# A residual that takes its natural row order by a trip through HBM, in a one-layer encoder kernel

## The chip, the cores and the metric

The kernel runs on one core of a Trainium2 chip. A core has TensorE (PE, matrix products; its weight loads are listed as PEld), VectorE (DVE), ScalarE (ACT), GpSimd (POOL) and SyncE (SP), which run at once, each through its own instructions in order, and tie to each other by semaphores. SBUF is the memory on the chip with 128 partitions, PSUM takes the products of TensorE, and DMA queues move data between SBUF and HBM. The metric is the time of one execution in microseconds on the device; less is better.

## The reference, cut to what matters

One layer: a mixing sub-layer (recurrent branch and attention, merged by gates), then a feed-forward sub-layer. What touches the change is the last part:

```python
mix_out = jnp.einsum("bsd,de->bse", merged, w_out[layer])
x = x + rms_norm(mix_out, mix_norm_post[layer])
h = rms_norm(x, ffn_norm_pre[layer])
up = jnp.einsum("bsd,df->bsf", h, w_up[layer])          # 1024 -> 2 x 3072
up = causal_dwconv(up, conv_f_w[layer], conv_f_b[layer])
gate, val = jnp.split(up, 2, axis=-1)
ffn_out = jnp.einsum("bsf,fd->bsd", jax.nn.gelu(gate) * val, w_down[layer])
x = x + rms_norm(ffn_out, ffn_norm_post[layer])
```

There are 512 tokens of width 1024, all in float32. Every norm is taken per token, so the order in which tokens lie in the partitions does not matter to it; the convolution runs along tokens and needs their order.

## The kernel before, in words

**Precision.** Every operand of a product is split into a rounded high half (written by ScalarE as a cast) and a low half (operand minus high half, mostly by VectorE). Three matmuls stand for one: high x high, high x low, low x high.

**Row order.** The host gives the tokens of each block of 128 in a turned order: partition a*64+i holds token 2i+a. All token-major tiles have that order, the residual `x2t` among them (four blocks of 128 tokens x 1024). Channel-major tiles come out of transposes; there the matmul reads its moving operand through `turns`, which restores the order of tokens. At the end the host puts the rows of the output back into natural order.

**Mixing, end.** `mix_norm` (L1232) takes one block of 128 tokens through the post-norm, adds the residual into `x2t` (L1247, VectorE) and goes on to the pre-norm of the feed-forward part. The blocks run at about 512 to 547 us.

**Up-projection** (about 566 to 757 us of the span). 24 pairs of weight tiles (one of the gate half, one of the value half). The first three are done plainly, the others with seven products in place of eight (a Strassen scheme), one pair per call of `period` (L480), some 9.4 us each. A pair's `raw_up` weights (2 x 512 KB) are loaded by SyncE's queue, L374, three pairs ahead (`load`, L1504). The low halves `ml` of its plain weights are made by a DMA: ScalarE writes the negated rounding (L390), and POOL's queue adds the weight to it (L391, an accumulating DMA, 512 KB for the first tile, 256 KB for half of the second). A load takes over the SBUF of the pair two before, so it waits until that pair's `ml` DMAs have landed. The product gate x value, `yf`, is made on POOL (L1378) and written to HBM as `yd` by SyncE's queue (L1379). The order within a period is written out by hand.

**Down-projection** (about 760 to 872 us). Again seven products in place of eight, of six steps each: 42 steps, each with two blocks of 128 tokens by two weight tiles, twelve matmuls of 512 columns. `prep(i)` (L1469) makes the four halves of step i: the weight's high half `wh_dn` on ScalarE (L198) and low half `wl_dn` on VectorE (L201), the gated product's high half `ah` on ScalarE (`y_hi`, L1464) and low half `al` on VectorE (`y_lo`, which goes through the helper `sub`, L351). It runs two steps ahead of `down_step` (L1478). From step 6 on the gated product's quarters `q` are combined by VectorE (L1574) first. In `y_hi` and `y_lo` the source is read through `parted`, which takes every second element, so that the product's columns, which are tokens, come into the turned order; then the output rows fit the order of `x2t`. The last product's second token block is done in halves of 256 columns.

**End.** Blocks of the result are folded together (L1605, L1688), squared and scaled, and `x2t` is added: for the blocks 2 and 3 by an accumulating DMA on POOL's queue (L1632), for the blocks 0 and 1 by VectorE (L1626). Then they go out.

Tile names end in running numbers, which the profile leaves out. A listing of instructions shows `ml_11` for the first low tile or the second of pair 11, by its size 128x1024 or 128x512.

Of the kernel before, what the change touches and what calls it, by code (L numbers as in the profile page):

```python
# [8 lines left out]
F32 = mybir.dt.float32  # L9
# [78 lines left out]
def kernel(  # L88
# [1111 lines left out]
    xpool = fstk.enter_context(tc.tile_pool(name="x2", bufs=1, reuse_waits="tile"))  # L1200
    x2t = xpool.tile([P, NT, D], F32, name="x2t")
    nc.sync.dma_start(x2t, xv)
    def out_matmuls(acc, toks, k, ah, al, wh, wl, nk, halves=(0, 1)):
        for t in toks:
            tok = slice(t * P, (t + 1) * P)
            for hf in halves:
                c = slice(512 * hf, 512 * hf + 512)
                dst = acc[t][hf]
                pe.matmul(dst, ah[:, tok], turns(wh[:, c], SH), start=k == 0, stop=False)
                pe.matmul(dst, ah[:, tok], turns(wl[:, c], SH), start=False, stop=False)  # L1210
                pe.matmul(dst, al[:, tok], turns(wh[:, c], SH), start=False, stop=k == nk - 1)
# [7 lines left out]
    with ExitStack() as mix:  # L1219
# [12 lines left out]
        def mix_norm(t, acc):  # L1232
            u = n2pool.tile([P, D], F32, tag="u", name=f"u{t}")
            xn = n2pool.tile([P, D], F32, tag="xn", name=f"xn2_{t}")
            s2 = small.tile([P, 2], F32, tag="s2", name=f"s2_mix{t}")
            for i, c in enumerate(HALVES):
                act.activation(out=xn[:, c], in_=acc[t][i], func=AF.Square, accum_out=s2[:, i : i + 1])
                dve.tensor_tensor(out=u[:, c], in0=acc[t][i], in1=gb[0][:, c], op=ALU.mult)
            yield
            ss = small.tile([P, 1], F32, tag="ss", name=f"ss_mix{t}")  # L1240
            dve.tensor_tensor(out=ss, in0=s2[:, 0:1], in1=s2[:, 1:2], op=ALU.add)
            rs = rstd_of(ss, f"mix{t}", eps4)
            if t > 1:
                yield
            s3 = small.tile([P, 2], F32, tag="s2", name=f"s2_f{t}")
            for i, c in enumerate(HALVES):
                dve.scalar_tensor_tensor(out=x2t[:, t, c], in0=u[:, c], scalar=rs, in1=x2t[:, t, c],  # L1247
                                         op0=ALU.mult, op1=ALU.add)
                act.activation(out=xn[:, c], in_=x2t[:, t, c], func=AF.Square, accum_out=s3[:, i : i + 1])
            yield  # L1250
            ss = small.tile([P, 1], F32, tag="ss", name=f"ss_f{t}")
            dve.tensor_tensor(out=ss, in0=s3[:, 0:1], in1=s3[:, 1:2], op=ALU.add)
            rs = rstd_of(ss, f"f{t}")
            for c in HALVES:
                scaled2[t] = dve.scalar_tensor_tensor(out=xn[:, c], in0=x2t[:, t, c], scalar=rs, in1=gb[1][:, c],
                                                      op0=ALU.mult, op1=ALU.mult)
            yield
            turned[t] = to_channels(xn, t, h2h, h2l, hf, "f")
# [195 lines left out]
        yraw[1, m] = ypool.tile([P, 2, SH], F32, tag="yr", name=f"yr{m}")  # L1454
        nc.sync.dma_start(yraw[1, m], yd[m][:, :, X])

    def tokens(y, order):
        return order(y.rearrange("p k c -> p (k c)"))

    def y_hi(i):  # L1460
        pl, b = (ypool, 3) if i < NS else (dpools[0], LATE)
        yhl[i] = [pl.tile([P, 2, SH], F32R, tag=f"a{x}", name=f"a{x}{i}", bufs=b) for x in "hl"]
        yhl[i].append(yraw[STEPS[i]])
        act.copy(tokens(yhl[i][0], placed), tokens(yhl[i][2], parted))  # L1464

    def y_lo(i):
        sub(tokens(yhl[i][1], placed), tokens(yhl[i][2], parted), tokens(yhl[i][0].bitcast(F32), placed))

    def prep(i):  # L1469
        if i < len(STEPS):  # L1470
# [31 lines left out]
    pairs.update({j: none for j in (JF, JF + 1, JF + 2)})  # L1502

    def load(j):  # L1504
        if NU < j < JF - 3:
            pairs[j + 3] = up_pair(j + 3)
        elif j == JF - 2:
            for i in range(2):
                load_w(i)
                load_first(i)  # L1510
# [286 lines left out]
```

## Time and profile before

| What | Value |
|---|---|
| median of three runs | 887.05 us (886.27 to 887.78) |
| the profiled execution | 886.33 us |
| its span | 884.6 us, 15833 instructions |
| PE, DVE, ACT, POOL busy | 98%, 84%, 69%, 24% of the span |
| DMA | 185.24 MB, 209 GB/s in the mean |

The span runs from the first to the last instruction; the execution's time has 1.7 us more. A group row ends in busy time, mean ns of one, idle time before and what ended it. A row of the timeline gives start, duration, engine, line, operation and tiles, and in brackets the engine's idle time ahead of it with what ended that. A DMA's time to landing runs from its issue to its semaphore. Ends of matmuls are modelled, so starts are compared here.

### The profile page before, as it was taken

Reading aid. Unit: us, or ns where it says so; the run is one execution under the profiler, and the core shown is the slowest. Engines: PE = TensorE matmul, PEld = TensorE weight load, DVE = VectorE, ACT = ScalarE, POOL = GpSimd, SP = SyncE. Lnnn points to the kernel's source line nnn. Section 1 sums busy time; section 2 is a strip of 40 time slices with the busy share of each in tenths; the row PEclk is TensorE's granted clock in tenths of the full one; section 3 lists DMA queues with packets and bytes.
Section 4 is the critical chain, followed back from the end, with each engine's and each line's share of the span. In section 5 each row is a group of like instructions: output and inputs, shape, how many; then the busy total and the mean of one; then the engine's idle time right before and its main releaser. Section 6 shows DMA issues by size and latency. Waiting matters only on the chain.

```text
span 884.6 us, 15833 instructions
## 1 busy us (share of the span) xinstructions
PE 871.0 (98%) x5856; PEld 794.5 (90%) x5856; DVE 744.6 (84%) x1209; ACT 611.1 (69%) x1031; POOL 215.4 (24%) x278
## 2 busy tenths in 40 slices
PE   9999999999999999999999999999999999999996
PEld 7888888888899988888888889999999999988885
DVE  7986469738978849998868699999999999889997
ACT  6575595533466648776755497888888888688774
POOL 3344334536011013121104100233332332100000
PEclk9999999999999999999999999999999999999999
DMA  7787689999874377353506663778898898699864
GB/s 268 231 273 220 172 228 258 238 277 197 192 182 135 116 261 274 132 171 129 202 26 202 218 200 107 175 183 236 217 222 244 211 226 208 223 399 307 276 192 149
DMA packets 71040, 185.24 MB, mean 209 GB/s; under 512 B 7153, under 2 KB 27681, under 8 KB 70578
## 3 DMA queue, kind: packets, MB, share of 16 engines
q1 hardware_dynamic: 47360, 127.72, 43.2%
q0 software_dynamic: 23456, 56.37, 29.3%
q8 instruction: 46, 0.75, 0.3%
q14 instruction: 32, 0.26, 0.1%
q10 hardware_dynamic: 146, 0.14, 0.0%
HBM read 150.69 MB, written 35.73 MB: 211 GB/s over the span
## 4 chain that ended last, share of the span: by engine, by line
PE 85%; DVE 9%; ACT 2%; issue 2%; DMA 1%; DVEq 0%; SPq 0%; ACTq 0%
PE up L458 7%; PE up L456 7%; PE up L455 7%; PE dn L1500 2%; PE dn L1499 2%; PE dn L1498 2%; PE ga L245 2%; PE ga L244 2%; PE ga L246 2%; DVE al L351 2%; PE pa L245 2%; PE pa L244 2%; PE v L335 2%; PE v L336 2%; PE xa L244 2%
## 5 line engine op out<-in xcount | busy, mean ns | idle before, releaser
L1370 DVE SCALAR_TENSOR_TENSOR u<-up,cpt,u 128x511 f32<-128x511 f32 x96 | 71.3, 745 | 3.5 <-ACT u L1364 1.8
L391 POOL DMA_DIRECT2D ml<-raw_up x42 | 36.2, 861 | 148.1 <-ACT ml L390 88.8
L1500 PE MATMUL dn<-wh_dn,al 128*128 128x512 f32 (+1 forms) x180 | 66.5, 369 | 1.2 <-DVE al L351 1.2
L1499 PE MATMUL dn<-wl_dn,ah 128*128 128x512 f32 (+1 forms) x180 | 66.2, 368 | 0.5 <-DVE wl_dn L201 0.4
L1498 PE MATMUL dn<-wh_dn,ah 128*128 128x512 f32 (+1 forms) x180 | 65.7, 365 | 0.0
L455 PE MATMUL up<-sh,th 128*128 128x256 f32 x252 | 59.5, 275 | 0.0
L456 PE MATMUL up<-sl,th 128*128 128x256 f32 x252 | 59.5, 275 | 0.0
L201 DVE TENSOR_TENSOR wl_dn<-raw_dn,wh_dn 128x1024 fp32r<-128x1024 f32 x42 | 51.1, 1217 | 5.0 <-ACT wh_dn L198 5.0
L351 DVE TENSOR_TENSOR tl<-t,th 128x1024 fp32r<-128x1024 f32 x42 | 51.1, 1218 | 0.0
L1364 ACT ACTIVATE u<-up,cpt 128x512 f32<-128x512 f32 x48 | 36.9, 778 | 19.9 <-PE up L458 10.0
L455 PEld LDWEIGHTS up<-sh,th 128*128 128x128 f32 x252 | 48.4, 192 | 0.0
L456 PEld LDWEIGHTS up<-sl,th 128*128 128x128 f32 x252 | 48.4, 192 | 0.0
L198 ACT CAST wh_dn<-raw_dn 128x1024 fp32r<-128x1024 f32 x42 | 44.3, 1054 | 4.7 <-DMA raw_dn<-td 2.8
L437 ACT CAST th<-t 128x1024 fp32r<-128x1024 f32 x42 | 43.8, 1045 | 2.6 <-DVE t L351 0.6
L1378 POOL TENSOR_TENSOR yf<-u,u 128x512 f32<-128x512 f32 x23 | 30.4, 1323 | 58.8 <-issue 46.0
L1500 PEld LDWEIGHTS dn<-wh_dn,al 128*128 128x128 f32 x180 | 34.1, 189 | 7.5 <-DVE al L351 3.5
L456 PE MATMUL up<-h2l,mh 128*128 128x256 f32 x168 | 39.7, 275 | 0.0
L455 PE MATMUL up<-h2h,mh 128*128 128x256 f32 x168 | 39.7, 275 | 0.0
L1499 PEld LDWEIGHTS dn<-wl_dn,ah 128*128 128x128 f32 x180 | 34.1, 189 | 6.0 <-DVE wl_dn L201 1.8
L1054 ACT ACTIVATE P<-P,mx 128x384 f32<-128x384 f32 (+3 forms) x64 | 35.2, 552 | 5.1 <-DVE mx L1049 5.1
L458 PE MATMUL up<-sh,tl 128*128 128x256 f32 x252 | 38.4, 275 | 0.0
L1498 PEld LDWEIGHTS dn<-wh_dn,ah 128*128 128x128 f32 x180 | 34.1, 189 | 4.0
(729 smaller groups left out, 3230.2 us busy)
## 6 DMA issues: line engine op xcount, KB each, us to landing
raw_up<-in_w_up_dram SPq DMA_DIRECT2D x48, 512.0 KB, 5.3
td<-in_w_down_dram POOLq DMA_DIRECT2D x36, 512.0 KB, 7.1
raw_dn<-td SPq DMA_DIRECT2D x24, 512.0 KB, 4.9
ml<-raw_up POOLq DMA_DIRECT2D x21, 512.0 KB, 5.3
B<-cnd POOLq DMA_DIRECT2D x16, 640.0 KB, 5.4
raw_dn<-in_w_down_dram SPq DMA_DIRECT2D x18, 512.0 KB, 4.2
raw_wo<-in_w_out_dram SPq DMA_DIRECT2D x16, 512.0 KB, 4.2
td<-td POOLq DMA_DIRECT2D x12, 512.0 KB, 12.5
```

The lines of the kernel that those rows point to most:

```text
L198: act.copy(self.wh, self.raw)
L201: engine.tensor_tensor(out=self.wl, in0=self.raw, in1=self.wh.bitcast(F32), op=ALU.subtract)
L244: pe.matmul(dst, ah, bh, start=first, stop=False)
L351: dve.tensor_tensor(out=out, in0=a, in1=b, op=ALU.subtract)
L437: act.copy(self.th[i], self.t[i])
L455: pe.matmul(dst, wh[:, k], turns(ah[:, k]), start=first and k == 0, stop=False, skip_group_check=True)
L456: pe.matmul(dst, wh[:, k], turns(al[:, k]), start=False, stop=False, skip_group_check=True)
L458: pe.matmul(dst, wl[:, k], turns(ah[:, k]), start=False, stop=k == KH - 1, skip_group_check=True)
L1370: dve.scalar_tensor_tensor(out=c[:, s:], in0=ps[:, : S - s], scalar=col(C_CFW + 3 * e + j), in1=c[:, s:], op0=ALU.mult, op1=ALU.add)
L1498: pe.matmul(d[:, x], ah[:, k, tok], bh, start=first, stop=False, skip_group_check=True)
L1499: pe.matmul(d[:, x], ah[:, k, tok], bl, start=False, stop=False, skip_group_check=True)
L1500: pe.matmul(d[:, x], al[:, k, tok], bh, start=False, stop=last, skip_group_check=True)
```

## The change: what it does

When `mix_norm` has made a block of `x2t`, POOL's queue writes it to a new HBM tensor `x2d`, in two DMAs of 64 partitions (the even and the odd tokens), each to every second row, so that `x2d` holds the tokens in natural order. In the up-projection, in the period of pair 9 (`j == NU + 6`), POOL's queue reads it back into `x2t` in four DMAs of 512 KB. `y_hi` and `y_lo` copy and subtract without `parted` and `placed`, in natural order. The end then adds residual and result in natural order, and the host no longer turns the rows of the output.

```diff
+    x2d = ctx.enter_context(tc.tile_pool(name="x2d", bufs=1, space=bass.MemoryType.DRAM)).tile([S, D], F32, name="x2d")
+    x2n = x2d.rearrange("(t i a) d -> t a i d", a=2, i=HT)
+
+    def x2_out(t):
+        for a in range(2):
+            nc.gpsimd.dma_start(x2n[t, a], x2t[HT * a : HT * (a + 1), t])
+
+    def x2_back():
+        for t in range(NT):
+            nc.gpsimd.dma_start(x2t[:, t], x2d[t * P : (t + 1) * P])
...
                 act.activation(out=xn[:, c], in_=x2t[:, t, c], func=AF.Square, accum_out=s3[:, i : i + 1])
+            x2_out(t)
             yield
...
-    def tokens(y, order):
-        return order(y.rearrange("p k c -> p (k c)"))
-
     def y_hi(i):
...
-        act.copy(tokens(yhl[i][0], placed), tokens(yhl[i][2], parted))
+        act.copy(yhl[i][0], yhl[i][2])
 
     def y_lo(i):
-        sub(tokens(yhl[i][1], placed), tokens(yhl[i][2], parted), tokens(yhl[i][0].bitcast(F32), placed))
+        sub(yhl[i][1], yhl[i][2], yhl[i][0].bitcast(F32))
...
     def load(j):
+        if j == NU + 6:
+            x2_back()
         if NU < j < JF - 3:
             pairs[j + 3] = up_pair(j + 3)
...
-    rows = r.results[0]["out_0_dram"].reshape(NT, 2, HT, D)
-    return rows.transpose(0, 2, 1, 3).reshape(1, S, D)
+    return r.results[0]["out_0_dram"][None]
```

On PE, DVE and ACT the instructions and their order stay as they were. On POOL twelve DMAs come in. At the end of the mixing part, POOL's instructions before and then with the change (`tg` is the merge ahead of it):

```order
L1194 TENSOR_TENSOR tg_5679<-tg_5679,pa 128x512
L391 DMA ml_3_6553<-raw_up_6460 128x1024
L391 DMA ml_3_6558<-raw_up_6461 128x512
L391 DMA ml_4_6758<-raw_up_6539 128x1024
```

```order
L1194 TENSOR_TENSOR tg_5679<-tg_5679,pa 128x512
L1208 DMA x2d<-x2t 64x1024 x8
L391 DMA ml_3_6564<-raw_up_6471 128x1024
L391 DMA ml_3_6569<-raw_up_6472 128x512
L391 DMA ml_4_6769<-raw_up_6550 128x1024
```

The eight writes stand between the merge and the first low tile of the up-projection. In the up-projection, around pair 11, before and with the change:

```order
L391 DMA ml_10_7630<-raw_up_7462 128x512
L391 DMA ml_11_7679<-raw_up_7596 128x1024
L1378 TENSOR_TENSOR yf_7735<-u_7675,u_7635 128x512
L391 DMA ml_11_7765<-raw_up_7597 128x512
L391 DMA ml_12_7814<-raw_up_7731 128x1024
```

```order
L391 DMA ml_10_7641<-raw_up_7473 128x512
L391 DMA ml_11_7690<-raw_up_7607 128x1024
L1212 DMA x2t<-x2d 128x1024 x4
L1390 TENSOR_TENSOR yf_7750<-u_7686,u_7646 128x512
L391 DMA ml_11_7780<-raw_up_7608 128x512
L391 DMA ml_12_7829<-raw_up_7746 128x1024
```

The four reads come in behind the first low tile of pair 11 and ahead of the gated product `yf` and of the second low tile. On SyncE's queue the order stays, but the two loads of pair 13 change what they wait for; these rows are the loads of pairs 12 and 13 with their waits (DMASW are the semaphores of POOL's DMAs, DMAHW those of SyncE's), before and with the change:

```order
L374 DMA raw_up_7731<-in_w_up_dram 128x1024 [waits DMASW7_49,DMAHW7_49,DVE_49,Activation_49]
L374 DMA raw_up_7732<-in_w_up_dram 128x1024 [waits DMAHW5_49,DMAHW6_49,DMASW6_49,DVE_49]
L1379 DMA yd_6741<-yf_7735 128x512 [waits Pool_49]
L374 DMA raw_up_7866<-in_w_up_dram 128x1024 [waits DMASW1_49,DMAHW2_49,DVE_49,Activation_49]
L374 DMA raw_up_7867<-in_w_up_dram 128x1024 [waits DMAHW0_49,DMAHW1_49,DMASW0_49,DVE_49]
```

```order
L374 DMA raw_up_7746<-in_w_up_dram 128x1024 [waits DMASW7_49,DMAHW7_49,DVE_49,Activation_49]
L374 DMA raw_up_7747<-in_w_up_dram 128x1024 [waits DMAHW5_49,DMAHW6_49,DMASW6_49,DVE_49]
L1391 DMA yd_6752<-yf_7750 128x512 [waits Pool_49]
L374 DMA raw_up_7881<-in_w_up_dram 128x1024 [waits DMASW0_49,DMAHW1_49,DVE_49,Activation_49]
L374 DMA raw_up_7882<-in_w_up_dram 128x1024 [waits DMAHW0_49,DMAHW2_49,DMASW5_49,Activation_49]
```

Before, the first load of pair 13 waits for the second low tile of pair 11 (DMASW1) and the second load for its first (DMASW0). With the change it is the other way round: the first load waits for the first low tile (DMASW0), which lands earlier, and the second load for the second (now DMASW5).

## The prediction

> **What bounds the kernel now.** I read the busy times and the chain of waits on the page first, then stretches of the span, then the rows of the stages that the change touches.
>
> ```profile
> PE 871.0 (98%) x5856; PEld 794.5 (90%) x5856; DVE 744.6 (84%) x1209; ACT 611.1 (69%) x1031; POOL 215.4 (24%) x278
> PE 85%; DVE 9%; ACT 2%; issue 2%; DMA 1%; DVEq 0%; SPq 0%; ACTq 0%
> ```
>
> TensorE is the bound almost everywhere, so a term counts only if it lengthens or shortens a wait of TensorE, or the tail behind its last matmul. Three stretches (span, then busy time and count of PE, PEld, DVE, ACT, POOL; clock; DMA share; GB/s) show where there is such a wait: the up-projection, the middle of the down-projection, and its last steps.
>
> ```profile
> 566.00:757.00 191.00, 191.00 (x1713) 191.00 (x1713) 178.55 (x264) 157.07 (x241) 60.86 (x61) 1.00 0.86 217
> 784.00:861.00 77.00, 77.00 (x364) 67.55 (x362) 73.25 (x91) 61.49 (x78) 0.85 (x1) 1.00 0.85 282
> 861.00:871.60 10.60, 9.37 (x43) 6.66 (x42) 10.24 (x16) 7.96 (x13) 0.56 (x1) 1.00 0.48 137
> ```
>
> In the up-projection and from 784 to 861 TensorE never stops: 77.00 us for 364 matmuls of 512 columns are 0.212 us each. From 861 to 871.6 it does only 43 in 10.60 us, and by the code 12 of them are half as wide (step 37's second token block, 256 columns). At the pace before, 31 x 0.212 + 12 x 0.11 = 7.9 us would have done. So TensorE loses 10.6 - 7.9 = 2.7 us there, and these rows of the timeline say to whom:
>
> ```profile
> 861.08 0.46 PE L1499 MATMUL dn<-wl_dn,ah 128*128 128x512 f32 x1
> 861.73 0.48 PE L1500 MATMUL dn<-wh_dn,al 128*128 128x512 f32 x1 [0.19 <-DVE al L351]
> 862.05 0.38 PE L1498 MATMUL dn<-wh_dn,ah 128*128 128x512 f32 x1
> 866.49 0.48 PE L1500 MATMUL dn<-wh_dn,al 128*128 128x512 f32 x1 [0.16 <-DVE al L351]
> 868.22 0.48 PE L1499 MATMUL dn<-wl_dn,ah 128*128 128x512 f32 x1 [0.39 <-DVE wl_dn L201]
> 868.87 0.48 PE L1500 MATMUL dn<-wh_dn,al 128*128 128x512 f32 x1 [0.16 <-DVE al L351]
> 870.67 0.48 PE L1500 MATMUL dn<-wh_dn,al 128*128 128x512 f32 x1 [0.19 <-DVE al L351]
> 767.13 0.48 PE L1500 MATMUL dn<-wh_dn,al 128*128 128x512 f32 x1 [0.36 <-DVE al L351]
> 775.56 0.48 PE L1500 MATMUL dn<-wh_dn,al 128*128 128x512 f32 x1 [0.16 <-DVE al L351]
> ```
>
> Each time it waits for VectorE, which makes the low halves: `al` of the gated product and `wl_dn` of the weight. The bracket understates a wait. From 861.08 to 861.73 are 0.65 us where 0.21 would do, and the next start is 0.32 behind: 0.44 + 0.11 = 0.55 us for a bracket of 0.19. The two early rows (steps 1 and 4) are the same kind of wait: 0.36 + 0.16 in the brackets, and by that measure up to 0.55 each.
>
> **The change part by part: the two copies of the gated product.** Both now read and write rows in order; before, the read took every second element. Groups of the same trace, by form (mean ns of one behind the comma):
>
> ```profile
> L1464 ACT CAST ah<-q 128x512 fp32r<-128x512 f32 x36 | 31.4, 871 | 5.5 <-DVE q L1574 4.6 <-DVE q L351 0.5 <-DMA q<-yd 0.3
> L406 ACT CAST mh<-raw_up 128x512 fp32r<-128x512 f32 x21 | 12.8, 608 | 0.0
> L351 DVE TENSOR_TENSOR al<-q,ah 128x512 fp32r<-128x512 f32 x36 | 29.5, 820 | 0.0
> L1300 DVE TENSOR_TENSOR sl<-hf,sh 128x512 fp32r<-128x512 f32 x8 | 5.1, 687 | 0.0
> L1574 DVE SCALAR_TENSOR_TENSOR q<-q,q 128x512 f32<-128x512 f32 x18 | 12.2, 676 | 0.0
> ```
>
> The unstrided row of the same operation and size is 608 ns on ScalarE and 687 on VectorE, and 676 for a VectorE operation of the same stage. So I take 871 - 608 = 263 ns off each `ah` and 820 - 687 = 133 ns off each `al`: over 36 steps 9.5 us of ScalarE and 4.8 us of VectorE. ScalarE's share lies beside other work. VectorE's matters: from 784 to 861 it is busy 73.25 of 77 us. By step 37 some 30 copies have saved 30 x 0.133 = 4.0 us, more than the 2.7 us by which TensorE is held up afterwards. I take all 2.7 us. What could hold it back is the chain through ScalarE and the tail:
>
> ```profile
> 859.77 1.23 DVE L201 TENSOR_TENSOR wl_dn<-raw_dn,wh_dn 128x1024 fp32r<-128x1024 f32 x1 [1.62 <-ACT wh_dn L198]
> 877.99 0.42 DVE L1688 TENSOR_TENSOR kept<-dn,kept 128x256 f32<-128x256 f32 x1
> 876.89 0.28 PE L1500 MATMUL dn<-wh_dn,al 128*128 128x256 f32 x1
> 865.71 0.72 DVE L351 TENSOR_TENSOR al<-q,ah 128x512 fp32r<-128x512 f32 x1
> ```
>
> At 859.77 VectorE itself waits for ScalarE, which had waited for VectorE's row scale of a finished token block; that scale is read in order behind `al`, so it comes earlier by the same 4 us and the wait moves with it. The tail's last fold (877.99) starts behind VectorE's own queue, 0.8 us after the last matmul ends, so it follows VectorE's gain and not TensorE's alone. For the two early waits I take 0.8 us: at step 4 ScalarE's 263 ns and VectorE's two copies of 133 (0.53 together) cover the wait; at step 1 `al` runs beside GpSimd and little is sure. **Gain: 2.7 + 0.8 = 3.5 us.** Bounds: at the least the five late brackets alone, 1.1 us, and at the most VectorE's whole 4.8 us.
>
> The Trainium skill, on SBUF — State Buffer, section "Door 1: The DMA port swizzle (why `[64,N]` ≈ `[32,N]`)", says that SBUF is fetched in lines of 16 bytes and that a stride of up to four fp32 costs nothing; a stride of two would then be free and this gain nil. The groups above disagree (871 against 608, 820 against 687).
>
> **The residual written out.** Eight DMAs on POOL's queue, 2 MB, each waiting for VectorE's `x2t` of its token block.
>
> ```profile
> POOL ml L391 <- DVE sl L1300: 58.5, 1, 58.5
> 515.00:525.00 10.00, 10.00 (x72) 8.26 (x71) 10.00 (x17) 8.76 (x15) 0.00 (x0) 1.00 0.62 209
> 535.00:545.00 10.00, 9.40 (x103) 8.96 (x102) 9.16 (x18) 5.04 (x14) 0.00 (x0) 1.00 0.27 78
> ```
>
> POOL stands idle for 58.5 us there, so nothing queues behind the issues; the DMA engines are busy 0.62 where the first two blocks go out and 0.27 where the last two do. 209 GB/s at 0.62 busy are 337 GB/s while busy, so 1 MB takes 3.1 us, which the free 0.38 x 10 = 3.8 us hold; nobody waits for the writes until the read-back, 90 us later. I put it at 0, and at 0.5 us if a weight load of that stage is pushed back.
>
> **The read-back.** Four DMAs, 2.1 MB, behind the low weight tile of pair 11 on POOL's queue, in the middle of the up-projection. Nothing needs `x2t` until the end, but the transfer stands in front of others:
>
> ```profile
> 630.46 0.86 POOL L391 DMA_DIRECT2D ml<-raw_up  x1 [4.18 <-ACT ml L390]
> 631.66 1.57 SPq L374 DMA_DIRECT2D raw_up<-in_w_up_dram  x2
> 633.50 1.28 POOL L1378 TENSOR_TENSOR yf<-u,u 128x512 f32<-128x512 f32 x1 [2.19 <-issue]
> 639.03 1.07 ACT L390 ACTIVATE ml<-raw_up 128x1024 fp32r<-128x1024 f32 x1 [0.43 <-DMA raw_up<-in_w_up_dram]
> 640.40 0.86 POOL L391 DMA_DIRECT2D ml<-raw_up  x1 [4.79 <-ACT ml L390]
> ml<-raw_up POOLq DMA_DIRECT2D x1, 512.0 KB, 4.9
> 649.23 0.61 PE L458 MATMUL up<-h2h,ml 128*128 128x256 f32 x4
> 630.00:635.20 5.20, 5.20 (x49) 5.20 (x48) 4.78 (x8) 4.38 (x8) 2.55 (x3) 1.00 0.75 116
> 635.20:640.00 4.80, 4.80 (x46) 4.80 (x45) 4.73 (x8) 3.70 (x7) 0.40 (x1) 1.00 1.01 324
> SPq L374 <- DMA ml<-raw_up: 116.3, 19, 8.1
> 640.00:641.50 1.50, 1.50 (x16) 1.50 (x15) 1.46 (x3) 1.50 (x3) 0.86 (x1) 1.00 0.09 18
> L1633 POOL DMA_DIRECT2D out_dram<-o x1 | 0.6, 562 | 4.1 <-DMA o<-x2t 4.1
> ```
>
> Issue: 4 x 0.56 us fit between 631.3 and `yf` at 633.50, so POOL's queue is not late. Transfer: 2.1 MB at the 324 GB/s of the busy stretch are 6.5 us, at the page's fastest slice (399) 5.3; I take 5.7 us of all engines. Two things stand behind it. The loads of 631.66 (pair 12) share the engines with it; one of the four ahead of the first tile makes it 5.7 / 4 = 1.4 us later. ScalarE already waits 0.43 us for that tile at 639.03, but has 191 - 157 = 34 us idle in 191, 1.7 us in each period of 9.4, to catch up in, so I count nothing for it. The next low tile (issued 640.40, landed 4.9 us later at 645.3, first read by TensorE at 649.23) has 3.9 us to spare; against it stand 5.7 us less the 1.4 us in which the engines now idle (640 to 641.5, 0.09 busy) = 4.3, and a weight load of pair 13 (0.52 MB, 1.6 us) that the new order lets go earlier, ahead of it. TensorE then waits 0.4 to 2.0 us, once. I take the upper half, **1.5 us**. Bounds: 0 if the idle shares of neighbouring periods absorb it, 5.7 if nothing does. If a wait comes, the same matmul (L458 on `ml`) has it, and the periods behind move with it.
>
> **Sum.** The profiled execution took 886.33 us at a span of 884.6. 886.33 - 3.5 + 1.5 = 884.3; against the median of 887.05, which stands 0.7 us above the profiled one, 887.05 - 2.0 = 885.0 us. A measurement of this kernel can tell 0.2%, 1.8 us, from no change.
>
> **The rivals.** *The read-back is hidden* (for: the engines are busy 0.86 in the up-projection, so 1.3 us of each 9.4 us period are free; against: the 3.9 us of slack is shorter than 5.7). Then 887.05 - 3.5 = 883.5.
> *The copies do not get faster, or VectorE's gain is stopped elsewhere*: the strided pace would come from two engines at one tile and not from the stride. For: `al` at 865.71 takes 0.72 us, strided. Against: eight and more unstrided rows at 676 to 687. Then the gain is 0 to 1.5 against the same 1.5: 887.0 to 888.5. The rule of the Trainium skill on SBUF — State Buffer ("Door 1", above) would give this case.
> *Slower*: the up-projection has no slack at all, since each load waits for the low tile's DMA (116.3 us in 19 times on SyncE's queue), which waits for ScalarE, which waits for a load (639.03). Then the backlog runs round this loop and TensorE pays it whole: 887.05 - 3.5 + 5.7 = 889.2. It decides from a wait of 3.5 us in the up-projection on, and can be told from no change at 5.3. Against: 1.4 us stand idle every 9.4.
>
> **How the numbers follow.** The forecast 0.47, own range 884.0 to 886.2; hidden 0.28; no gain 0.15; slower 0.10. Range 882.9 to 887.8: it takes in the first two and part of the third, and leaves the slower case and a gain near 4.8 out. Faster by over 0.2% (under 885.3): nearly all of hidden and 0.3 of the forecast's 0.47, 0.57. Within: 0.33. Slower: 0.10.
>
> **What would show it.** In the profile after: `ah` near 608 and `al` near 687 ns; no brackets for `al` or `wl_dn` between 861 and 871; VectorE still saturated or freed in 784 to 861; one wait on L458 within 15 us behind the read-back, for a DMA of `ml`; the low tile's time to landing near 9 us there instead of 4.9. Copies still near 871 and 820 would make the gain wrong, a TensorE without a gap in the up-projection the cost, and a gap over 3.5 us the sign.

## The result, and the profile after

The changed kernel takes 888.5 us in the median of 20 runs (886.5 to 889.1), the kernel before 886.8 us in as many (885.3 to 887.9): a ratio of 1.0017, 95% interval 1.0010 to 1.0023. That is 1.7 us more, where 885.0 [882.9 to 887.8] was forecast: outside the range, on its slow side, at the upper end of what the rival of no gain gave (887.0 to 888.5, chance 0.15), and just inside the 0.2% within which the text called it no change. The profiled execution took 886.99 us at a span of 885.1, 1.5 us under its median, so costs are read from places in the trace and their sums are held against medians.

Busy times and the chain of waits by engine, from the page of the kernel after:

```profile
PE 871.1 (98%) x5856; PEld 796.0 (90%) x5856; DVE 740.4 (84%) x1209; ACT 600.5 (68%) x1031; POOL 220.6 (25%) x290
PE 80%; DVE 10%; ACT 3%; DMA 3%; issue 3%; DVEq 0%; ACTq 0%
```

ScalarE has lost 10.6 us of work and VectorE 4.2, close to the 9.5 and 4.8 forecast. TensorE's share of the chain has fallen from 85% to 80%, and DMA's has risen from 1% to 3%: the transfers have moved onto the path. Groups of the down-projection by form (mean ns of one behind the comma):

```profile
L1473 ACT CAST ah<-q 128x512 fp32r<-128x512 f32 x36 | 22.1, 614 | 1.5 <-DVE q L351 1.1 <-DVE q L1585 0.2
L351 DVE TENSOR_TENSOR al<-q,ah 128x512 fp32r<-128x512 f32 x36 | 24.7, 686 | 0.0
```

The copies have the pace that was forecast (608 and 687). Yet it pays little in the middle. The same stretches as before, in the kernel after (busy time and count of PE, PEld, DVE, ACT, POOL; clock; DMA share; GB/s):

```profile
566.00:757.00 191.00, 189.62 (x1694) 189.12 (x1693) 178.11 (x261) 156.54 (x239) 61.85 (x64) 1.00 0.88 225
784.00:861.00 77.00, 77.00 (x358) 67.56 (x358) 70.42 (x92) 55.12 (x78) 0.85 (x1) 1.00 0.84 294
861.00:871.60 10.60, 10.35 (x58) 8.47 (x57) 10.31 (x14) 7.54 (x14) 0.56 (x1) 1.00 0.53 149
```

The up-projection has a hole now, and TensorE is full from 784 to 861 as before. From 861 to 871.6 it does 58 matmuls where it did 43, but they are not the same ones: TensorE comes there 2.4 us later in this trace. So the same matmuls are compared next.

**Where the time went.** For every kernel of this study I take the start of the same matmul (by its place in TensorE's order, which is the same in all of them) in its trace and in that of the kernel before. The difference is the shift; its change across a stretch is what the stretch costs (+) or gains (-). The columns lie, in the time of the kernel before, at 525 to 550 us (end of the mixing part), 550 to 642, 642 to 762 (from just behind the read-back's place), 762 to 860 (down-projection), and 860 to the end of the span. All in us, one execution each. Where neither kernel differs, the columns move by up to 0.3. In 762 to 860 the three kernels whose early copies are strided as before move by 0.03 to 0.12; those with the same copies in order differ among themselves, from -0.7 to +0.2 (the read-back at the end on POOL's queue apart).

| kernel | 525-550 | 550-642 | 642-762 | 762-860 | 860-end |
|---|---|---|---|---|---|
| after | +1.01 | +0.19 | +1.92 | -0.31 | -1.87 |
| after, a second profile | +2.59 | +0.21 | +1.46 | -0.62 | -1.84 |
| copies alone | -0.08 | +0.09 | 0.00 | +0.21 | -1.86 |
| natural in steps 0-25 alone | -0.19 | +0.31 | 0.00 | -0.68 | +0.03 |
| natural in steps 26-41 alone | +0.23 | +0.11 | 0.00 | -0.12 | -1.85 |
| trip alone | +1.67 | 0.00 | +2.15 | -0.03 | +0.10 |
| write-out alone | +1.05 | +0.28 | 0.00 | -0.10 | 0.00 |
| late write-out | +0.25 | +0.09 | +6.25 | -0.31 | -1.86 |
| late write-out, second profile | -0.04 | +0.98 | +7.14 | -0.16 | -1.84 |
| reads behind the loads | +1.51 | 0.00 | +2.79 | -0.56 | -2.09 |
| late write-out, reads behind the loads | -0.05 | +0.98 | +5.38 | -0.68 | -2.11 |
| half the read-back | +1.60 | +0.24 | +0.57 | -0.24 | -1.32 |
| late write-out, one block per period | +0.49 | +0.83 | +2.78 | +0.11 | -1.87 |
| read-back at the end, POOL's queue | -0.07 | +0.54 | 0.00 | +2.90 | -1.65 |
| read-back at the end, SyncE's queue | +0.02 | +0.40 | 0.00 | -0.49 | -1.94 |
| strided weight load, no trip | -0.06 | +0.20 | 0.00 | -0.45 | -1.87 |
| strided weight load, quarter trip | +0.03 | 0.00 | 0.00 | -0.64 | -1.28 |

Three places carry it: the write-out, the read-back, and the last 25 us.

**The write-out.** DMA issues between 513.5 and 517 us, before and then after (KB each, us from issue to landing):

```profile
raw_wo<-in_w_out_dram SPq DMA_DIRECT2D x1, 512.0 KB, 3.4
```

```profile
x2d<-x2t POOLq DMA_DIRECT2D x4, 256.0 KB, 4.9
raw_wo<-in_w_out_dram SPq DMA_DIRECT2D x1, 512.0 KB, 5.9
```

and two rows of ScalarE's timeline after, with TensorE's first matmul behind the mixing part; the last row is that matmul before:

```profile
520.72 1.06 ACT L198 CAST wh_wo<-raw_wo 128x1024 fp32r<-128x1024 f32 x1 [1.86 <-DMA raw_wo<-in_w_out_dram]
523.05 1.05 ACT L198 CAST wh_up<-raw_up 128x1024 fp32r<-128x1024 f32 x1 [1.27 <-DMA raw_up<-in_w_up_dram]
545.69 0.38 PE L256 MATMUL up<-h2h,wh_up 128*128 128x256 f32 x1 [0.75 <-ACT hf L293]
```

```profile
545.06 0.38 PE L256 MATMUL up<-h2h,wh_up 128*128 128x256 f32 x1 [0.65 <-ACT hf L293]
```

The weight load `raw_wo` shares the engines with the first writes and takes 2.5 us longer. ScalarE waits 1.86 and 1.27 us for weights, for which it did not wait before:

```profile
520.14 1.05 ACT L198 CAST wh_wo<-raw_wo 128x1024 fp32r<-128x1024 f32 x1 [0.92 <-PE wo L1211]
521.22 1.04 ACT L198 CAST wh_up<-raw_up 128x1024 fp32r<-128x1024 f32 x1
```

The norms of the last blocks stand in its queue behind these casts, and TensorE waits for the norms: by 545 its shift has gone from -0.37 to +0.63. The chain of waits that leads to the matmul at 545.69 goes back to a load, the next one behind `raw_wo`; before, at that time it ran over TensorE's own matmuls:

```profile
517.28 5.74 DMA raw_up<-in_w_up_dram
523.05 1.05 ACT wh_up L198
```

ScalarE is late from 520 on, before the last two blocks are written (from 537.08 on). So in this trace it is the writes of the first two blocks that cost.

**The read-back.** The chain of waits between 640 and 660 us (start, length), and TensorE's two waits:

```profile
641.92 9.90 DMA ml<-raw_up
651.87 0.71 PE up L458 x4
```

```profile
649.38 0.71 PE L458 MATMUL up<-sh,ml 128*128 128x256 f32 x4 [0.50 <-DMA ml<-raw_up]
651.87 0.71 PE L458 MATMUL up<-h2h,ml 128*128 128x256 f32 x4 [0.89 <-DMA ml<-raw_up]
```

Place and kind are as forecast: the matmul L458 waits for low tiles, though 18 and 20 us behind the reads and not within 15. The first wait is for the second low tile of pair 11, whose DMA stands right behind the reads on POOL's queue, the second for the first low tile of pair 12. The first of these DMAs, before and after:

```profile
ml<-raw_up POOLq DMA_DIRECT2D x1, 256.0 KB, 7.3
```

```profile
ml<-raw_up POOLq DMA_DIRECT2D x1, 256.0 KB, 13.8
```

The second took 9.9 us where it took 4.9. The first load of pair 12, issued among the reads at 632.58, landed after 7.9 us where it took 7.3. So it is the low tiles behind the reads that are late, far more than the load. Against TensorE the tile of pair 12 goes out 0.7 us later and lands 5.0 us slower; less its 3.9 us of slack that leaves 1.8, about what the table shows.

**The down-projection.** Why 4.2 us less work on VectorE give 1.9 us shows in its low weight tile of step 26 and of step 37, after (two rows each of ScalarE and VectorE):

```profile
828.48 0.59 ACT L1613 COPY kept<-dn 128x512 f32<-128x512 f32 x1 [2.27 <-PE dn L1509]
829.77 0.58 ACT L1613 COPY kept<-dn 128x512 f32<-128x512 f32 x1 [0.70 <-PE dn L1509]
831.34 1.23 DVE L201 TENSOR_TENSOR wl_dn<-raw_dn,wh_dn 128x1024 fp32r<-128x1024 f32 x1 [2.19 <-ACT wh_dn L198]
860.61 1.23 DVE L201 TENSOR_TENSOR wl_dn<-raw_dn,wh_dn 128x1024 fp32r<-128x1024 f32 x1 [1.62 <-ACT wh_dn L198]
```

and the row of step 26 before:

```profile
828.91 1.23 DVE L201 TENSOR_TENSOR wl_dn<-raw_dn,wh_dn 128x1024 fp32r<-128x1024 f32 x1 [0.18 <-ACT wh_dn L198]
```

ScalarE has two copies of a finished product (`kept`, L1613) in its queue there, and these wait for TensorE's last matmul into it. `wh_dn` stands behind them and VectorE waits for `wh_dn`: 2.19 us where it was 0.18. Whatever VectorE has saved up to step 26 it waits away, since TensorE itself has not become faster. From this row to that of step 37 it takes 29.27 us where it took 30.86 (828.91 to 859.77), 1.6 us less for 11 steps, and 0.3 less in the steps behind. That does not cover all of TensorE's late waits. No bracket is left for them, but some starts are still too far apart:

```profile
868.51 0.38 PE L1507 MATMUL dn<-wh_dn,ah 128*128 128x512 f32 x1
868.91 0.48 PE L1508 MATMUL dn<-wl_dn,ah 128*128 128x512 f32 x1
869.51 0.48 PE L1509 MATMUL dn<-wh_dn,al 128*128 128x512 f32 x1
869.83 0.38 PE L1507 MATMUL dn<-wh_dn,ah 128*128 128x512 f32 x1
870.69 0.44 PE L1508 MATMUL dn<-wl_dn,ah 128*128 128x512 f32 x1
871.24 0.48 PE L1509 MATMUL dn<-wh_dn,al 128*128 128x512 f32 x1
```

From 868.51 on these are 0.40, 0.60, 0.32 and later 0.55 us to the next start, where 0.22 would do. Counted so, TensorE lost 3.0 us between 861 and 872 before and still loses 1.1.

### The profile page after: what moved, and what is told of

Read it like the earlier page. It is cut to its first block, busy times and chain, and to the rows that moved or that the text cites. A ratio compares the mean times of both kernels' runs of the same rounds, so it can differ in the third digit from the quotient of the medians.

```text
span 885.1 us, 15847 instructions
## 1 busy us (share of the span) xinstructions
PE 871.1 (98%) x5856; PEld 796.0 (90%) x5856; DVE 740.4 (84%) x1209; ACT 600.5 (68%) x1031; POOL 220.6 (25%) x290
## 4 chain that ended last, share of the span: by engine, by line
PE 80%; DVE 10%; ACT 3%; DMA 3%; issue 3%; DVEq 0%; ACTq 0%
PE up L458 6%; PE up L456 6%; PE up L455 6%; PE dn L1509 2%; PE ga L246 2%; PE ga L244 2%; PE ga L245 2%; PE dn L1508 2%; PE dn L1507 2%; DMA raw_up<-in_w_up_dram 2%; PE pa L245 2%; PE pa L244 2%; PE xa L244 2%; PE v L335 2%; PE xa L245 2%
## 5 line engine op out<-in xcount | busy, mean ns | idle before, releaser
L458 PE MATMUL up<-sh,tl 128*128 128x256 f32 x252 | 38.5, 275 | 0.0
```

Source lines behind the costliest of these rows:

```text
L458: pe.matmul(dst, wl[:, k], turns(ah[:, k]), start=False, stop=k == KH - 1, skip_group_check=True)
```

## The experiments

### Do the copies' savings add up?

Copies alone, without the trip:

```diff
-            x2_out(t)
...
-        if j == NU + 6:
-            x2_back()
```

> The changed kernel without the two trips: the gated product is copied in natural order, nothing is written to x2d or read back, and x2t keeps its turned order (so the residual is added to the wrong token of its block; the work is the same otherwise). Theory of the prediction, that the VectorE time saved by all copies adds up: 3.5 us less than before. Theory of the lead, made from the trace of the changed kernel: VectorE can only run as far ahead of TensorE as the weight buffers let it; it is at that limit at step 26 (wl_dn there waits 2.19 us for ScalarE, which waits for TensorE), so only what the copies save from there on counts: 11 steps of 0.13 to 0.14 us and 0.28 us in the last ones, 1.6 + 0.3 = 1.9, and 0.1 early: 2.0 us less. If the copies gained nothing at all in the end: 0.

Measured: 884.6 us against 887.0 (0.9978, 0.9969 to 0.9988): 2.0 us less by the ratio.

The first 26 steps and the last 16, apart (the diff is against the copies alone):

```diff
-        act.copy(yhl[i][0], yhl[i][2])
+        if i < 26:        # the other kernel: i >= 26
+            act.copy(yhl[i][0], yhl[i][2])
+        else:
+            act.copy(tokens(yhl[i][0], placed), tokens(yhl[i][2], parted))
...
```

(the same in `y_lo`).

> The kernel before with natural order in the copies of steps 0 to 25 of the down-projection alone (their products come out in natural token order and the others in turned order, so the output mixes them; times only). No trip. Prediction's theory, saved time adds up: 26 x 0.133 = 3.5 us of VectorE, enough for all of the 2.7 us late waits: 2.7 to 3.5 us less. Theory of the lead: VectorE's head start is cut at step 26 by the weight buffers: 0 to 0.3 us less.

> The kernel before with natural order in the copies of steps 26 to 41 alone (output mixed as in the run with the first 26). No trip. Prediction's theory: 16 x 0.133 = 2.1 us of VectorE at the most, less where the last strided copies take only 0.72: 1.4 to 2.1 us less, and the first 26 alone more than that. Theory of the lead: all of the gain, 1.7 to 2.0 us less, within 0.3 us of the kernel that copies in order everywhere.

Measured: the first 26 give 886.4 (0.9996, 0.9987 to 1.0005), no gain that the time can tell; the last 16 give 885.2 (0.9979, 0.9970 to 0.9987), all of it within the error. VectorE's row of step 26 in the one with the first 26:

```profile
828.73 1.23 DVE L201 TENSOR_TENSOR wl_dn<-raw_dn,wh_dn 128x1024 fp32r<-128x1024 f32 x1 [2.44 <-ACT wh_dn L198]
```

It waits 2.44 us and starts where it started before (828.91). So the theory of the added savings falls and the lead is what counts. What the first 26 do give is small and comes at the two early waits: at step 1 TensorE gains 0.23 us in every profile with the early copies in order and nothing in the three without, and behind step 4 the gain is 0.05 to 0.6 in all. Two profiles lose it again at step 5, copies alone among them, where ScalarE waits 1.47 us for a load. One detail of my expectation was wrong: at step 26 the limit is the copy of the finished product in ScalarE's queue, not the weight buffers; those set ScalarE's later waits for TensorE (0.8 to 1.0 us per step at 837 to 846).

### What does the trip cost?

The trip alone, in the kernel before (rows kept in turned order in HBM, so that the output fits), and the write-out alone:

```diff
+    x2n = x2d.rearrange("(t a i) d -> t a i d", a=2, i=HT)    # trip alone; write-out alone: "(t i a) d"
...
+            x2_out(t)
...
+        if j == NU + 6:        # trip alone
+            x2_back()
```

> The kernel before with the trip of the residual alone: the same eight writes and four reads at the same places, but the rows keep the turned order in HBM, and the copies stay strided as before. Theory of the prediction: 1.5 us more (the write-out free). From the profiled execution of the changed kernel: 1.0 for the write-out and 1.8 for the read-back, 2.8 us more there; but the median of the changed kernel lies 1.5 us above its profiled execution, so if the trip is what varies it should cost 3.5 to 4.3 us in the median, with a spread of more than 2 us between executions.

> The kernel before with the write-out alone: eight writes of x2t to x2d at the end of the mixing part; nothing reads x2d, no read-back, the copies strided. Prediction: 0 (at most 0.5 us). From the traces of the changed kernel and of the run with the trip alone, where the weight loads raw_wo and raw_up landed late and TensorE's starts moved back by 1.0 and 1.7 us between 540 and 548 us: 1.0 to 1.7 us more than before. A rival, that the read-back pays all of the 3.9 us of the trip and the early shift is chance: 0 here.

Measured: the trip 890.9 against 887.0 (1.0044, 1.0031 to 1.0056), 3.9 us more; the write-out 888.2 against 886.9 (1.0019, 1.0010 to 1.0027), 1.7 us more by the ratio (1.3 by the medians and by its trace). The write-out is not free, and 2.2 us are left for the read-back, as the trip's trace has it (+2.15). With the copies' -2.0 the sum is +1.9; the changed kernel has +1.5 to +1.7 here and +1.2 to +1.4 when measured again.

The changed kernel once more:

> The changed kernel once more, word for word, for a second profile of it: its profiled execution was 1.5 us under its median. Expected: 888.2 to 888.8 in the median; in the profile the write-out moves TensorE's starts by 1.0 to 1.7 us at 540 to 548 us and the read-back by 1.8 to 2.5 at 645 to 655, or by more than 4 where all four reads stand ahead of the first weight load of pair 12.

Measured: 888.4 against 887.0 (1.0014, 1.0004 to 1.0023). Its profile has the write-out dearer (+2.59) and the read-back at +1.46. The stretches behind the write-out show why:

```profile
536.00:541.00 5.00, 3.60 (x42) 3.23 (x40) 4.16 (x9) 3.14 (x10) 2.12 (x4) 1.00 0.59 153
541.00:546.00 5.00, 5.00 (x42) 4.88 (x40) 5.00 (x8) 2.25 (x4) 0.00 (x0) 0.66 0.73 247
```

TensorE idles 1.4 us, and then has a granted clock of 0.66 in the mean of 5 us. One of the two profiles has that second cost and the other not, so it is one thing that can make executions of this kernel differ.

### Can the trip be put where it costs nothing?

Write-out two DMAs per period, in the first four periods of the up-projection; the read-back as in the changed kernel:

```diff
-            x2_out(t)
...
     def load(j):
+        if j < NU + NT:
+            x2_out(j - NU)
```

> The changed kernel with its write-out moved: two of the eight writes in each of the first four periods of the up-projection (behind the low tile on POOL's queue), where the engines are busy 0.57 to 0.83; the read-back as it is. If the write-out costs because it comes in one burst beside loads that TensorE soon needs: its 1.0 to 1.7 us go away, copies -2.0 and read-back +2.1 to 2.2 remain: 0 to 0.5 us more than before, 1.2 to 1.7 less than the changed kernel. If any 2 MB of writes cost that much wherever they are: the same as the changed kernel (+1.7 over before).

Measured: 889.2 against 886.9 (1.0029, 1.0013 to 1.0046), not less than the changed kernel, where 1.2 to 1.7 us less was expected. Its executions lie in two groups, 885.7 to 887.3 and 891.1 to 892.2, with two between. The profiled one is of the second. The write-out itself cost what was forecast, almost nothing (+0.25, +0.09); the read-back cost 6.25. ScalarE and TensorE there, and two stretches:

```profile
645.79 1.06 ACT L390 ACTIVATE ml<-raw_up 128x1024 fp32r<-128x1024 f32 x1 [5.54 <-DMA raw_up<-in_w_up_dram]
649.51 0.38 PE L455 MATMUL up<-sh,th 128*128 128x256 f32 x1 [4.36 <-DVE up L474]
645.00:650.00 5.00, 0.64 (x6) 0.49 (x5) 2.15 (x4) 4.21 (x7) 1.22 (x2) 1.00 1.07 327
650.00:655.00 5.00, 5.00 (x32) 5.00 (x32) 4.93 (x8) 3.68 (x8) 1.75 (x2) 0.66 1.05 275
```

ScalarE waits 5.54 us for a weight load, TensorE 4.36, and then the clock is 0.66 in the mean of 5 us, in which TensorE's shift grows by another 1.7 us. The Trainium skill, on TensorE: Matmul & The Clock Gate, section "Part 1: The HAM clock gate (the "warmup" mystery)", says that after an idle window of some 3.4 us the array runs at half clock until it has been busy for about as long; the 4.36 us pause and the slow stretch after it agree. The 1.4 us of idle time in the second profile of the changed kernel, with the same 0.66 behind, do not fit that figure.

Issues of SyncE and POOL at that place, in the changed kernel and then in this one:

```profile
631.83 2.47 POOL L1212 DMA_DIRECT2D x2t<-x2d  x4
632.58 1.67 SPq L374 DMA_DIRECT2D raw_up<-in_w_up_dram  x2
```

```profile
633.27 2.46 POOL L1212 DMA_DIRECT2D x2t<-x2d  x4
635.21 1.26 SPq L374 DMA_DIRECT2D raw_up<-in_w_up_dram  x2
```

In the changed kernel the load is issued among the reads, here behind all four. A second profile of the same kernel, to see whether that order decides:

> The kernel with the late write-out once more, for one profile: its twelve executions lay in two groups, five of 885.7 to 887.3 and five of 891.1 to 892.2, and the profiled one was of the slow group, with all four reads issued ahead of the first weight load of pair 12. If the order decides between the groups: a profile of the fast group has that load ahead of two or more of the reads and a wait of less than 1 us; one of the slow group has it behind all four again and a wait of some 4 us. If neither holds, the order is not the cause.

Measured: one execution of 893.6 us, the order as in the first (load at 636.64, last read issued at 635.55), TensorE's wait 4.23 us and a clock of 0.50 behind it. An execution of the other group was not profiled. So I turned the order round: reads on SyncE's queue behind both loads of pair 12, once in the changed kernel, once with the late write-out.

```diff
-            nc.gpsimd.dma_start(x2t[:, t], x2d[t * P : (t + 1) * P])
+            nc.sync.dma_start(x2t[:, t], x2d[t * P : (t + 1) * P])
...
             pairs[j + 3] = up_pair(j + 3)
+            if j == NU + 6:
+                x2_back()
```

> The changed kernel with the four reads on SyncE's queue directly behind the two weight loads of pair 12, and so behind both instead of among them; nothing else is moved. Theory that the order of issue sets the price (in the changed kernel two of four reads stand ahead of the first load and it lands after 7.9 us; in the run with the late write-out all four do, it lands after 10.5 us and TensorE waits 4.4 us): the loads land after 7 to 8 us again, ScalarE does not wait for them, only the low tiles behind the reads are late: 0.5 to 1.5 us less than the changed kernel. Theory that 5.7 us of transfer in a stretch with 1.3 us to spare per period cost the same in any order: the same as the changed kernel, 888.2 to 888.8.

> The kernel with the late write-out, its four reads now on SyncE's queue behind the two weight loads of pair 12 (so none of them can be ahead of the first load). If the order against that load causes the slow group of the kernel with the late write-out (891 to 892): no execution above 889.5, and a median of copies -2.0, write-out 0, read-back +1.4 to +2.7: 0.6 less to 0.7 us more than before, some 2 us under the kernel with the late write-out (889.2). If the slow group has another cause: executions of 891 to 892 again, and a median near 889.

Measured: 888.9 against 887.0 (1.0016, 1.0007 to 1.0026), the same as the changed kernel within the error; and 889.6 against 886.3 (1.0044, 1.0030 to 1.0058), where 885.7 to 887.0 was expected. The theory of the order falls. In the second, at the next pair:

```profile
644.14 0.84 SPq L374 DMA_DIRECT2D raw_up<-in_w_up_dram  x2
654.03 1.06 ACT L390 ACTIVATE ml<-raw_up 128x1024 fp32r<-128x1024 f32 x1 [5.62 <-DMA raw_up<-in_w_up_dram]
657.76 0.38 PE L455 MATMUL up<-sh,th 128*128 128x256 f32 x1 [3.33 <-DVE up L474]
```

The loads of pair 12 are on time, and the load of pair 13 is the one that lands 9.8 us after its issue. The backlog goes to whichever load stands behind it; the order only chooses which.

What the two pairs of kernels do show is that the read-back is dearer where the write-out was late: 6.25 and 7.14 against 1.92 and 1.46, and 5.38 against 2.79. The loads show how much reserve there is. Less TensorE's shift at 642, the first load of pair 12 goes out at 631.8 in the changed kernel (632.58 - 0.82) and 631.7 before, but at 634.5 (635.21 - 0.67 and 636.64 - 2.14) in the kernel with the late write-out and at 633.8 (634.25 - 0.43) in the last one. By the order of the program nothing else differs up to there. The two kernels below with the late write-out and no read-back in this stage have 633.7 (634.02 - 0.28 and 634.60 - 0.90), so the read-back is not what delays that load. The writes of 570 to 610 us push the loads back against TensorE by 2 to 3 us. TensorE feels 0.1 to 1.0 of it, since loads run ahead of it, and in 30 us the lead has not come back. The read-back then meets TensorE with less in hand. That is read from seven profiles; why single executions of the late write-out come out at 886 stays open.

One block per period, from pair 9 to pair 12:

```diff
+        if NU + 6 <= j < NU + 6 + NT:
+            x2_back(j - NU - 6)
```

> As the kernel with the late write-out, and the read-back taken apart too: one block of 512 KB (1.4 us of all engines) in each of the periods of pairs 9 to 12, in place of four at once. Theory of the burst: in each period 1.3 us of the engines are free (0.86 busy of 9.4 us), so each block costs at most 0.1 to 0.5 us and TensorE's waits at L458 go away: 1.5 to 2.0 us less than before. Theory that the up-projection has no slack (each load waits for the low tile of the pair before): the delays add up all the same, 0 to 0.5 us more than before.

Measured: 888.2 against 886.9 (1.0017, 1.0000 to 1.0034). Spreading does not bring the 1.5 to 2.0 us under the kernel before that the first theory had: the delays add up over the periods (+2.78 to 762), as the second theory had it.

Half the read-back (blocks 0 and 1), the accumulating DMAs of the end taking blocks 2 and 3 from HBM:

```diff
-        for t in range(NT):
+        for t in range(2):
...
-            nc.gpsimd.dma_start(os[t], x2t[:, t], accum_op=ALU.add)
+            nc.gpsimd.dma_start(os[t], x2d[t * P : (t + 1) * P], accum_op=ALU.add)
```

> The changed kernel with half the read-back at the same place: blocks 0 and 1 only (two DMAs of 512 KB), while the accumulating DMAs of blocks 2 and 3 in the end add their rows from x2d in HBM (in the run with the read-back at the end this cost nothing that could be seen). Write-out as in the changed kernel. If the up-projection absorbs a fixed 3 to 4 us of the 5.7: the halved read-back of 2.9 us is free, and 1.8 to 2.5 us less than the changed kernel, 886.0 to 886.6. If it passes on a share of whatever comes: 0.9 to 1.3 us less, 887.1 to 887.5.

Measured: 887.2 against 886.9 (1.0003, 0.9994 to 1.0012), 1.2 us under the changed kernel (888.4 when last measured, beside 887.0 for the kernel before). By the time the up-projection passes on a share and has no fixed reserve; by the trace, 0.57 us against 1.46 to 2.15, less than half. Between the two forms this does not decide; that a smaller read-back costs much less is clear.

### Versions without the cost

Late write-out, half the read-back, moved to the down-projection (steps 28 to 31), on POOL's queue (its two lines stand with a minus in the next diff):

> As the kernel with the late write-out, and the read-back halved and moved to the end: the accumulating DMAs of blocks 2 and 3 add their rows from x2d in HBM and not from x2t, and blocks 0 and 1 come back in four DMAs of 256 KB at steps 28 to 31 of the down-projection, where the engines are busy 0.65 to 0.74. With both bursts gone only the copies' gain should be left: 2.0 us less than before (by the prediction's own sum without the trip, 3.5 less). If the reads hold up the last weight loads or the accumulating reads from HBM are slow: 0 to 1 less.

Measured: 887.4 against 886.9 (1.0006, 0.9997 to 1.0014). It lost time at another place:

```profile
776.72 2.18 POOL L1211 DMA_DIRECT2D x2t<-x2d  x4
794.75 0.48 PE L1505 MATMUL dn<-wh_dn,ah 128*128 128x512 f32 x1 [1.34 <-ACT ah L1471]
```

The reads stand at step 28 in the program, but POOL has nothing to wait for and issues them at 777 us, into the fullest stretch of all (DMA share 1.03 at 775 to 785 in the kernel before). Moved to SyncE's queue, whose weight loads wait for buffers, they come out at 851 to 860:

```diff
-            nc.gpsimd.dma_start(x2t[:, t, c], x2d[t * P : (t + 1) * P, c])
+            nc.sync.dma_start(x2t[:, t, c], x2d[t * P : (t + 1) * P, c])
...
-            extra[28 + i].append(lambda i=i: x2_back(i // 2, HALVES[1 - i % 2]))
+            extra[33 + i].append(lambda i=i: x2_back(i // 2, HALVES[1 - i % 2]))
```

> As the kernel with the late write-out and the read-back at the end, but the four half reads of blocks 0 and 1 stand on SyncE's queue between the last weight loads (steps 33 to 36), since POOL's queue, which has nothing else to wait for there, sent them off at 777 us in place of some 840, in front of the first products' loads, which made TensorE wait from 793 to 799. In that run the write-out cost nothing between 547 and 779 (shift of TensorE's starts -1.52 and -1.55 us). So: the copies' gain alone, 1.8 to 2.2 us less than before. If the accumulating DMAs from HBM in the end are slower than from SBUF: the tail grows by 0.5 to 1.

Measured: 886.0 against 887.0 (0.9984, 0.9976 to 0.9993): faster than both kernels, by less than the 1.8 to 2.2 expected.

The turning put into TensorE's weight load, no trip:

```diff
-            tok = slice(P * t, P * (t + 1))
+            tok = slice(t, 2 * P, 2)
```

> Natural copies, no trip, and the turning put into TensorE's weight load of the down-projection: it takes every second token of 256 (stride two) in place of 128 in a row. The rows of the output then stand in another order than the residual's (the residual is added to the wrong tokens; the work is the same otherwise). It asks for the price of a strided weight load: PEld takes 190 ns in a row. If the stride costs nothing or stays hidden behind the matmuls (212 ns each): 2.0 us less than before, as with the copies alone. If a strided load takes what strided copies take more (871 against 608, 40%): 266 ns each against 212, 504 loads of which 480 are seen: some 25 us more.

Measured: 884.8 against 887.0 (0.9966, 0.9953 to 0.9978). One group of the weight loads, by form:

```profile
L1506 PEld LDWEIGHTS dn<-wh_dn,ah 128*128 128x128 f32 x180 | 35.4, 197 | 2.9
```

197 ns in place of 189 to 190: the stride costs 7 ns on an engine that is hidden behind the matmuls of 512 columns. Behind 871 us, where many matmuls are half as wide, TensorE's starts slip by 0.4 us in this kernel and in the next one, and in none of the others. So the turned order could be had without a trip, if the residual fits. It does when halves of 64 partitions change places:

```diff
+    CROSS = [x2t[HT:, 0], x2t[:HT, 1]]
+
+    def x2_out(i):
+        nc.gpsimd.dma_start(x2d[i], CROSS[i])
+
+    def x2_back(i):
+        nc.sync.dma_start(CROSS[i], x2d[1 - i])
...
-            nc.gpsimd.dma_start(os[t], x2t[:, t], accum_op=ALU.add)
+            for b in range(2):
+                rows = slice(HT * b, HT * (b + 1))
+                nc.gpsimd.dma_start(os[t][rows], x2t[HT * (t - 2) : HT * (t - 1), 2 + b], accum_op=ALU.add)
```

> The version without strided copies and with a quarter of the trip: TensorE's weight load takes every second of 256 tokens, which cost nothing in the run with the strided load, so output block t of a half holds tokens 2i + t of its 256. The residual's halves of 64 partitions are matched to that: for blocks 2 and 3 by two accumulating DMAs of 64 partitions each, straight from x2t in SBUF; for blocks 0 and 1 two halves change places by way of HBM, 256 KB each, written in the first two periods of the up-projection and read back at steps 33 and 34 on SyncE's queue. Expected: the gain of the run with the strided load, 2.0 to 3.0 us less than before, 884.0 to 885.0; 0.5 more if the four small accumulating DMAs lengthen the tail.

Measured: 885.7 against 886.9 (0.9988, 0.9980 to 0.9997): faster than both kernels too, 1.2 us under the kernel before and 2.7 under the changed one, though short of the 884.0 to 885.0 expected. Its trace has no cost up to 762 and gains 1.28 behind 860, where most others gain some 1.85.

## Why the prediction was wrong

**The write-out, put at 0: this step failed.** It cost 1.7 us alone. The prediction set 3.1 us of transfer against 3.8 us of free engine time in 10 us and asked who waits for the writes. The free time lies in single pieces between loads (before, the DMA share is 0.00 from 514 to 516 and 0.98 from 517 to 518), and it is the loads beside the writes that somebody waits for: `raw_wo`, 5.9 us in place of 3.4, and the `raw_up` behind it, 5.7 in place of 3.5. The bound named for it (0.5 us "if a weight load is pushed back") had the right event at a third of its price, and the loads' readers were never traced to TensorE.

**The gain, put at 3.5: mis-sized, 2.0 measured.** Every row of it held (`ah` 614, `al` 686 ns). What failed was "by step 37 some 30 copies have saved 30 x 0.133 = 4.0 us, more than the 2.7": for these waits only the copies from step 26 on count. The text did name the wait that "moves with it" at step 37 (1.62 us, the same after), but not the one at step 26, where before only 0.18 us stood. The 2.7 us themselves were read a little low: the 43 matmuls of that window take in two at its edge, and by the starts TensorE lost 3.0, of which 1.9 came back. The 0.8 us of the two early waits came to 0.05 to 0.6.

**The read-back, put at 1.5: the mechanism was right, the size low.** Same matmul and landing time (9.9 us where 9 was forecast), 1.5 and 1.9 us in two profiles and 2.2 by the trip less the write-out. The low tile right behind the reads (13.8 us) was left out of the working, but the tile that it did name is the later one and sets the sum. The bounds of 0 to 5.7 were too narrow at the top, since a long wait lowers the clock as well: 6.25 and 7.14 were seen with the late write-out.

**The sum.** -2.0 + 1.7 + 2.2 = +1.9 us, measured +1.7. Of the distance from the forecast of -2.0 to that sum, 3.9 us, the write-out makes 1.7, the gain 1.5 and the read-back 0.7.

**The rivals.** "Hidden" is out. "The copies do not get faster" is out in its premise: 871 ns became 614 and 820 became 686. Nor was it two engines at one tile: of the 36 strided `al` rows before, the five beside which ScalarE did nothing took 757 to 842 ns (808 in the mean, the others 821), and those in order take 681 to 691 with ScalarE at work or not. The Trainium skill on SBUF — State Buffer, section "Door 1: The DMA port swizzle (why `[64,N]` ≈ `[32,N]`)", says that a stride of up to four fp32 is free. ScalarE and VectorE do not bear that out here; TensorE's weight load, at 197 against 190, comes near it. The rival's second half, a gain stopped elsewhere, is what happened in part. That the time came out at the end of its 887.0 to 888.5 is luck: its gain was 0 to 1.5 and its cost 1.5, and measured were 2.0 and 3.9. "Slower" gave the backlog that runs from load to load with nothing to absorb it; that loop is seen where reads behind the loads of pair 12 made those of pair 13 late, but in the changed kernel it took a third of the 5.7 us and not all. I gave that side too little, since two of the three terms could only cost.

## What to carry to other kernels

Work taken off an engine that runs ahead of the bound counts only from the last place where that engine is made to wait for the bound; look for the copy or buffer that ties them before adding savings up. A transfer is not hidden by a mean share of free engine time: ask which load lands later beside it, who reads that load, and how much lead that reader has, and know that a lead spent earlier in the same stage is not there for the next burst. A DMA on a queue that has nothing to wait for starts when the queue is free, not where it stands in the program.

## What the runs showed of the hardware

A pause of TensorE can cost twice: behind waits of 4.2 to 4.4 us the granted clock was 0.50 to 0.66 in the next 5 us (matmuls start 0.21 us apart in place of 0.11), worth 1.7 and 2.7 us; behind one of 3.3 us it was 0.76 from 660 to 665, worth 1.9; and once it was 0.66 behind only 1.4 us of idle time. A read by every second element, through a pattern of more dimensions, cost ScalarE 42% and VectorE 20% on 512 elements; these runs do not tell the stride from the pattern. A TensorE weight load with a plain stride of two cost 4%. With queues of POOL and SyncE both full, a load of 0.5 MB issued behind 2 MB of reads of the other queue landed 10.5 us after its issue, between the third and the fourth of the reads.
